# A two-layer diffusion trunk: the blocks of a triangular inverse through DRAM as diagonal halves in one orientation, and two modulation chunks on VectorE

## The chip, the cores and the metric

One core of a Trainium2 chip runs the whole program. The metric is device microseconds of one execution, the median of several runs. The core has five engines with a queue of instructions each, run in order: TensorE (PE, and PEld for its weight loads), VectorE (DVE), ScalarE (ACT), GpSimd (POOL) and SyncE (SP). SP, ScalarE and GpSimd also issue DMAs; sixteen DMA engines move the bytes.

## The reference, cut to what matters

A trunk of two layers over 256 positions of width 2048, beside 256 positions of context. The first layer mixes by windowed attention (8 query heads, 2 key-value heads) and by a gated delta rule (8 heads, two directions); the second by a Fourier transform. A gated feed-forward follows in both, and six modulation vectors per layer come from `c @ w_ada`. The delta rule solves a triangular system for each head, direction and chunk of the sequence:

```python
    m = jnp.where(strict, jnp.einsum('bhncd,bhnsd->bhncs', kb, kc) * decay, 0.0)
    rhs = jnp.concatenate([vc * bc[..., None], kb * jnp.exp(gc)[..., None]], axis=-1)
    sol = lax.linalg.triangular_solve(jnp.eye(DELTA_CHUNK, dtype=jnp.float32) + m, rhs,
                                      left_side=True, lower=True, unit_diagonal=True)
```

The first step of all is `mx = split(silu_c @ w_ada + b_ada)` and `h = modulate(rms_norm(x), mx[0], mx[1])`, for x and for the context.

## The kernel before, in words

**Matrix products.** Every weight tile is loaded by SP into `raw` (L188), split by ScalarE into a rounded part `whi` (L198) and by VectorE into the rest `wlo` (L204). TensorE multiplies both with the split activations (all its products are issued on L133). `raw` has 4 buffers, `whi` and `wlo` 4 each. The order on the queues is made by a scheduler that goes by the program's order; the program itself is paced by `clock[0]`, the time that the TensorE work issued so far should take. A generator that says `yield x` goes on once 1.2 x us of such work have been issued after it. So `yield` sets how much TensorE work lies between two steps.

**The front.** The first two modulation vectors of layer 0 are computed in 32 chunks (16 blocks k of 128 rows, shift and scale), each loaded in two halves. `WHO` says by a letter who does a chunk: `p`, TensorE with 8 products per half (each two instructions); `d`, VectorE with two multiply-and-reduce steps per half (L275), one for x and one for the context. `mod_k` (L447 to L455) then makes the modulated, split activations `hT` of block k, and `proj_k` multiplies them with the first weights. Chunks are issued two blocks ahead of `mod_k`, and `mod_k` one ahead of `proj_k`. The first product of a block in `proj_k` goes to 32 rows (`pab`). The other ten vectors (`ada_d`) are made by VectorE in the background, also on L275.

**The delta rule.** The heads are worked in four pairs g = 0 to 3, while the projections of the next pairs and of the attention run. `gdn_a(g)` builds the system `Z`, and copies its 32x32 diagonal blocks into `Zc` (L718 to L720, with a turn of direction 1's blocks by VectorE). The two 16x16 diagonal halves of each block are inverted by elimination on VectorE, with one half block per partition. To get from blocks laid over partitions to one half block per partition, `Zc` is stored to DRAM (`dz`, L722, ScalarE's queue) and read back in two loads (L731). The elimination (L737 to L742, 15 steps) makes `Y`. `Y` and its turned copy (L745) are stored to `dy` in four DMAs, two on ScalarE's queue and two on SP's (L750). `dy` is one DRAM tile for all pairs, cleared once at the start (L244 to L248), so that the halves off the diagonal are zero. `gdn_b(g)` reads both orientations back as whole blocks, `YD` (L762, ScalarE's queue), then reads Kt and Vt (L767, L768), and goes on with small 32x32 products: `pQ`, `pP` (the off-diagonal halves), and the larger blocks after them. In the profile `YZ` and `YD` have the name T (their buffers are T4).

**Attention.** `attend(0)` and `attend(1)` load the queries of a key-value head from DRAM on GpSimd's queue: `attend(0)` all four heads at once into an A buffer, `attend(1)` two and two into QCH buffers, which also hold the pairs' queries.

The change touches `WHO` (L60), the constants at L244, `gdn_a`, `gdn_b` and `attend`.

Of the kernel before, what the change touches and what calls it, by code (L numbers as in the profile page):

```python
# [58 lines left out]

WHO = 'pd' * 16  # L60
PRE = (4, 4, 4, 4)
# [11 lines left out]
def trunk(ctx: ExitStack, tc: tile.TileContext, a: dict, dbg=None, stop=None):  # L73
# [20 lines left out]
    def t4(shape, dt=F32):  # L94
        return T(shape, "T4", 2, dt)
# [147 lines left out]
    nc.gpsimd.dma_start(off16, a["k_off16"])  # L243
    dy = dr.tile([2, 2, 8, 4, 32, 32], F32, tag="dy", name="dy", bufs=1)  # L244
    zero = T([P, 512], "C2", 3)
    nc.gpsimd.memset(zero, 0.0)
    for i in range(2):
        nc.gpsimd.dma_start(dy[i].rearrange("d e b r c -> (d e b) (r c)").rearrange("a (b c) -> (a b) c", b=2), zero)  # L248
    smallr = C([P, 3, 16], "smallr")
# [383 lines left out]
    def bl(i, n=32):  # L633
        return slice(n * i, n * i + n)

    def gdn_a(g):
# [83 lines left out]
        V.transpose(Zc[:, 1].rearrange("p e f -> p (e f)"), Zd1.rearrange("p e f -> p (e f)"))  # L720
        dz = dr.tile([2, 8, 4, 32, 32], F32, tag="dz", name=f"dz{g}")
        S.dma_start(dz.rearrange("d e b r c -> (b r) (d e) c"), Zc.rearrange("p d e c -> p (d e) c"))  # L722
        YZ = t4([P, 4, 16, 16])
        Y2, Zi = YZ[:, 0:2], YZ[:, 2]
        Yf = Y2[:, 0].rearrange("p r c -> p (r c)")
        nc.gpsimd.memset(Yf, 0.0)
        nc.gpsimd.memset(Yf[:, 0:256:17], 1.0)
        yield LD1
        for s in range(2):
            sl = slice(16 * s, 16 * s + 16)  # L730
            S.dma_start(Zi[bl(s, 64)], dz[:, :, :, sl, sl].rearrange("d e b r c -> (d e b) r c"))  # L731

        V.tensor_tensor(out=Zc.rearrange("p d e c -> p (d e) c"), in0=Zc.rearrange("p d e c -> p (d e) c"),
                        in1=off16.unsqueeze(1).to_broadcast([P, 16, 32]), op=ALU.mult)
        yield LD2
        Y = Y2[:, 0]
        for k in range(15, 0, -1):  # L737
            tmp = YZ[:, 3].rearrange("p r c -> p (r c)")[:, (k % 4) * 64:(k % 4) * 64 + k * (16 - k)]
            tv = tmp.rearrange("p (r c) -> p r c", r=k)
            V.tensor_tensor(out=tv, in0=Zi[:, 0:k, k:k + 1].to_broadcast([P, k, 16 - k]),  # L740
                            in1=Y[:, k:k + 1, k:16].to_broadcast([P, k, 16 - k]), op=ALU.mult)
            V.tensor_tensor(out=Y[:, 0:k, k:16], in0=Y[:, 0:k, k:16], in1=tv, op=ALU.subtract)  # L742
            if k % 4 == 0:
                yield YSUB
        V.tensor_copy(Y2[:, 1], Y.rearrange("p r c -> p c r"))  # L745
        yield 1.5
        for i in range(2):
            for s in range(2):
                sl = slice(16 * s, 16 * s + 16)
                (S, nc.sync)[s].dma_start(dy[i][:, :, :, sl, sl].rearrange("d e b r c -> (d e b) r c"), Y2[bl(s, 64), i])  # L750
        heads.setdefault(g, {}).update(K=K, Q=Q, Z=Z, Zv=Zv, A=A, Zc=Zc, sc=(ner, dvs, so1, so2))

    def gdn_b(g):
# [7 lines left out]
        YD = t4([P, 2, 2, 8, 32])  # L761
        S.dma_start(YD.rearrange("p i d e c -> p (i d e) c"), dy.rearrange("i d e b r c -> (b r) (i d e) c"))  # L762
        if g == 0:
            Kt, Vt = H["Kt"], H["Vt"]
        else:
            Kt, Vt = ktok([P, 2, 4, HD]), vtok([P, 2, 4, HD])
            S.dma_start(Kt.rearrange("p h c d -> p h (c d)"), dKt[g])  # L767
            S.dma_start(Vt.rearrange("p h c d -> p h (c d)"), dVt[g])  # L768
        yield LD4
        pQ = sm()  # L770
        pQv = pQ.rearrange("p (d e f) -> p d e f", d=2, e=8)
# [232 lines left out]
    def attend(kv):  # L1004
        for hp in range(2):
            if kv == 0:
                if hp == 0:
                    q4 = at([P, 4, 256])
                    nc.gpsimd.dma_start(q4, dq[0])
                qT = q4[:, hp * 2:hp * 2 + 2]  # L1010
            else:
                qT = qch([P, 2, 256])
                nc.gpsimd.dma_start(qT, dq[kv][:, hp * 2:hp * 2 + 2])
            yield 3
# [519 lines left out]
```

## Time and profile before

| | us |
|---|---|
| median of 3 runs | 2500.32 (2495.74 to 2503.1) |
| profiled execution | 2498.01 |
| its span | 2496.2 |
| TensorE busy | 2382.9 (95%) |
| VectorE busy | 1791.7 (72%) |
| ScalarE busy | 1284.7 (51%) |

The front ends at about 185 us; the delta rule, the projections and the attention fill the time to about 750 us; the output projection, feed-forward, Fourier mixing and second feed-forward follow. In the rows below, a timeline row has start us, length us, engine, line, operation, out<-in, shapes, count, and in brackets the idle time before it and what ended it. A window row has the stretch, its length, the busy us of PE, PEld, DVE, ACT and POOL with their instructions, the granted TensorE clock (1.00 is full speed), the busy share of the DMA engines and GB/s. A row on waits has the engine and line that waited, what for, us in total, times, longest.

### The profile page before, as it was taken

The numbers are of one execution on the slowest core, as the hardware profiler recorded it, in microseconds if no ns is written. First come the engines' busy times: TensorE is split into PE (matmuls) and PEld (weight loads), VectorE is DVE, ScalarE is ACT, GpSimd is POOL, SyncE is SP. The second block draws the span as 40 slices with busy tenths as digits, with TensorE's granted clock in tenths as the row PEclk, the third lists the DMA queues.
The fourth block names the chain that finished last, engine by engine and source line by source line (L and its number), as shares of the span: only waits on it lengthen the run. The fifth ranks groups of instructions, "written<-read, shape, count | busy, mean of one in ns | idle before, by whom it ended". The sixth has DMA issues, their size and how long they took to land.

```text
span 2496.2 us, 39579 instructions
## 1 busy us (share of the span) xinstructions
PE 2382.9 (95%) x14536; PEld 1982.1 (79%) x14536; DVE 1791.7 (72%) x3379; ACT 1284.7 (51%) x2314; POOL 84.7 (3%) x106
## 2 busy tenths in 40 slices
PE   7999899988999999999999999799999999999997
PEld 6888688966778788888888887777888888888886
DVE  5889788877575787777777787878666666555566
ACT  5347345463755645444454545546554544445455
POOL 1000000000000100000000001002000000000001
PEclk8999999989999999999999999999999999999998
DMA  8885777668256589888888898586576777656665
GB/s 302 289 291 180 230 226 259 210 219 275 69 185 205 177 309 314 311 306 317 318 311 313 309 321 305 206 294 217 189 239 233 234 238 243 192 183 190 189 202 192
DMA packets 218483, 611.04 MB, mean 245 GB/s; under 512 B 68904, under 2 KB 69912, under 8 KB 217520
## 3 DMA queue, kind: packets, MB, share of 16 engines
q1 hardware_dynamic: 168016, 581.59, 68.4%
q10 hardware_dynamic: 46528, 15.21, 2.5%
q0 software_dynamic: 3744, 11.71, 1.4%
q8 instruction: 114, 1.87, 0.3%
q14 instruction: 81, 0.66, 0.1%
HBM read 595.03 MB, written 13.40 MB: 244 GB/s over the span
## 4 chain that ended last, share of the span: by engine, by line
PE 78%; DVE 8%; DMA 7%; ACT 3%; issue 3%; POOL 0%; ACTq 0%; DVEq 0%; POOLq 0%
PE acc L133 68%; PE sm L133 9%; DMA araw<-in_ada_d 3%; DVE wlo L204 2%; DVE araw L275 2%; DVE C L524 1%; DVE S L1169 1%; PE sm L1252 1%; DMA T<-dz 1%; DMA dy<-T 1%; DMA T<-dy 1%; ACT whi L198 1%; DMA araw<-in_w_dn 0%; DMA dz<-Zc 0%; DMA smallr<-in_smallr 0%
## 5 line engine op out<-in xcount | busy, mean ns | idle before, releaser
L198 ACT ACTIVATE whi<-raw 128x512 fp32r<-128x512 f32 (+1 forms) x1324 | 831.1, 630 | 895.7 <-DVE wlo L204 465.5
L204 DVE TENSOR_TENSOR wlo<-raw,whi 128x512 fp32r<-128x512 f32 (+1 forms) x1306 | 893.9, 692 | 482.9 <-ACT whi L198 480.3
L133 PE MATMUL acc<-whi,S 128*128 128x512 f32 x3312 | 1058.6, 397 | 6.6 <-ACT whi L198 5.4
L133 PEld LDWEIGHTS acc<-whi,S 128*128 128x128 f32 x3312 | 626.5, 189 | 142.8 <-ACT whi L198 5.8
L133 PE MATMUL acc<-wlo,S 128*128 128x512 f32 x1656 | 650.6, 393 | 2.0 <-DVE wlo L204 2.0
L275 DVE SCALAR_TENSOR_TENSOR araw<-araw,cb 128x1024 f32<-128x1024 f32 x320 | 389.1, 1218 | 33.8 <-DMA araw<-in_ada_d 33.1
L133 PEld LDWEIGHTS acc<-wlo,S 128*128 128x128 f32 x1656 | 313.6, 189 | 72.5 <-DVE wlo L204 3.4
L133 PE MATMUL acc<-S,whi 128*128 128x256 f32 x1152 | 221.3, 287 | 3.1 <-DVE C L524 3.0
L133 PEld LDWEIGHTS acc<-S,whi 128*128 128x128 f32 x1152 | 184.1, 192 | 4.0 <-issue 3.1
L133 PE MATMUL acc<-S,wlo 128*128 128x256 f32 x576 | 163.3, 284 | 2.0 <-DVE wlo L204 2.0
L133 PE MATMUL acc<-whi,ZT 128*128 128x512 f32 x384 | 122.0, 391 | 0.0
L133 PEld LDWEIGHTS acc<-S,wlo 128*128 128x128 f32 x576 | 110.8, 192 | 2.7 <-DVE wlo L204 2.6
L133 PE MATMUL acc<-whi,KCH 128*128 128x512 f32 x320 | 111.1, 404 | 1.1 <-ACT whi L198 1.1
L133 PE MATMUL acc<-whi,A 128*128 128x512 f32 x312 | 105.5, 393 | 0.0
L133 PE MATMUL acc<-whi,T 128*128 128x512 f32 x296 | 99.5, 392 | 0.0
L133 PE MATMUL acc<-wlo,KCH 128*128 128x512 f32 x192 | 78.7, 410 | 7.0 <-DVE wlo L204 6.8
L133 PEld LDWEIGHTS acc<-whi,ZT 128*128 128x128 f32 x384 | 72.2, 188 | 15.2
L133 PE MATMUL acc<-wlo,ZT 128*128 128x512 f32 x192 | 75.5, 393 | 0.2 <-POOL wlo L204 0.2
L133 PEld LDWEIGHTS acc<-whi,KCH 128*128 128x128 f32 x320 | 62.2, 195 | 15.1 <-ACT whi L198 1.5
L133 PE MATMUL acc<-wlo,T 128*128 128x512 f32 x176 | 68.9, 391 | 0.0
L133 PEld LDWEIGHTS acc<-whi,A 128*128 128x128 f32 x312 | 58.6, 188 | 11.9
L133 PEld LDWEIGHTS acc<-whi,T 128*128 128x128 f32 x296 | 55.6, 188 | 12.2
(442 smaller groups left out, 2638.0 us busy)
## 6 DMA issues: line engine op xcount, KB each, us to landing
raw<-in_w_gu SPq DMA_DIRECT2D x347, 512.0 KB, 4.3
araw<-in_ada_d SPq DMA_DIRECT2D x320, 512.0 KB, 4.8
raw<-in_w_dn SPq DMA_DIRECT2D x179, 512.0 KB, 4.6
raw<-in_w_att SPq DMA_DIRECT2D x40, 512.0 KB, 4.5
raw<-in_w_gdn SPq DMA_DIRECT2D x34, 512.0 KB, 4.6
raw<-in_w_out SPq DMA_DIRECT2D x30, 512.0 KB, 3.5
raw<-in_w_four SPq DMA_DIRECT2D x30, 512.0 KB, 4.3
ZT<-in_ada_s SPq DMA_DIRECT2D x24, 512.0 KB, 4.5
```

Of the source, the lines that this page charges most:

```text
L133: nc.tensor.matmul(out, l, r, start=start, stop=stop)
L198: S.activation(hi[:, :w], raw[:, c:c + w], AF.Copy)
L204: eng.tensor_sub(lo[:, :w], raw[:, c:c + w], hi[:, :w].bitcast(F32))
L275: V.scalar_tensor_tensor(out=junk, in0=w, scalar=1.0, in1=rows, op0=ALU.mult, op1=ALU.mult, accum_out=dst)
L524: V.scalar_tensor_tensor(out=ca[:, :, lo:hi], in0=pv[:, :, lo + o:hi + o], scalar=wconv[:, blk, j:j + 1], in1=ca[:, :, lo:hi], op0=ALU.mul ...
L1169: V.scalar_tensor_tensor(out=x[:, t, sl], in0=y[:, t, sl], scalar=r, in1=x[:, t, sl], op0=ALU.mult, op1=ALU.add)
L1252: nc.tensor.transpose(p[:, i * P:(i + 1) * P], hv[t][:, i * P:(i + 1) * P], ident)
```

## The change

The letters of `WHO` are changed so that chunks 12 and 28 (the shift of blocks 6 and 14) are `d` instead of `p`. `dy` is no longer cleared, and is one tile per pair; a constant of two columns, `half`, has 1 for partitions of a block's one half and 0 for the other, and the reverse. In `gdn_a` VectorE takes the diagonal halves out of `Zc` into `Zd`, the store carries these alone, and one load reads them, one contiguous row per partition. `Y` alone is stored, in one DMA on ScalarE's queue, without the turned copy and the pause of 1.5 before it. In `gdn_b` the load brings `Y`'s halves; ScalarE and VectorE write them into the two halves of the blocks with zeros beside them, and VectorE turns the blocks for the second orientation, with a pause of 1 after it. `attend(1)` loads its four heads at once, into a T4 buffer.

```diff
-WHO = 'pd' * 16
+WHO = ('pd' * 6 + 'dd' + 'pd') * 2
...
-    dy = dr.tile([2, 2, 8, 4, 32, 32], F32, tag="dy", name="dy", bufs=1)
-    zero = T([P, 512], "C2", 3)
-    nc.gpsimd.memset(zero, 0.0)
-    for i in range(2):
-        nc.gpsimd.dma_start(dy[i].rearrange("d e b r c -> (d e b) (r c)").rearrange("a (b c) -> (a b) c", b=2), zero)
+
+    half = C([P, 2], "half")
+    V.tensor_copy(half[:, 0:1], off16[:, 16:17])
+    V.tensor_scalar(half[:, 1:2], off16[:, 16:17], -1.0, 1.0, ALU.mult, ALU.add)
...
-        dz = dr.tile([2, 8, 4, 32, 32], F32, tag="dz", name=f"dz{g}")
-        S.dma_start(dz.rearrange("d e b r c -> (b r) (d e) c"), Zc.rearrange("p d e c -> p (d e) c"))
-        YZ = t4([P, 4, 16, 16])
-        Y2, Zi = YZ[:, 0:2], YZ[:, 2]
-        Yf = Y2[:, 0].rearrange("p r c -> p (r c)")
+        Zf = Zc.rearrange("p d e c -> p (d e) c")
+        Zd = T([P, 16, 16], "K1", 3)
+        V.tensor_scalar_mul(Zd, Zf[:, :, 0:16], half[:, 0:1])
+        V.scalar_tensor_tensor(out=Zd, in0=Zf[:, :, 16:32], scalar=half[:, 1:2], in1=Zd, op0=ALU.mult, op1=ALU.add)
+        dz = dr.tile([16, 4, 2, 16, 16], F32, tag="dz", name=f"dz{g}")
+        S.dma_start(dz.rearrange("e b s r c -> (b s r) e c"), Zd)
+        YZ = t4([P, 3, 16, 16])
+        Y, Zi = YZ[:, 0], YZ[:, 1]
+        Yf = Y.rearrange("p r c -> p (r c)")
...
-        for s in range(2):
-            sl = slice(16 * s, 16 * s + 16)
-            S.dma_start(Zi[bl(s, 64)], dz[:, :, :, sl, sl].rearrange("d e b r c -> (d e b) r c"))
+        S.dma_start(Zi.rearrange("p r c -> p (r c)"), dz.rearrange("e b s r c -> (e b s) (r c)"))
...
-        V.tensor_copy(Y2[:, 1], Y.rearrange("p r c -> p c r"))
-        yield 1.5
-        for i in range(2):
-            for s in range(2):
-                sl = slice(16 * s, 16 * s + 16)
-                (S, nc.sync)[s].dma_start(dy[i][:, :, :, sl, sl].rearrange("d e b r c -> (d e b) r c"), Y2[bl(s, 64), i])
+        dy = dr.tile([16, 4, 2, 16, 16], F32, tag="dy", name=f"dy{g}")
+        S.dma_start(dy.rearrange("e b s r c -> (e b s) (r c)"), Yf)
...
-        S.dma_start(YD.rearrange("p i d e c -> p (i d e) c"), dy.rearrange("i d e b r c -> (b r) (i d e) c"))
+        Yd = T([P, 16, 16], "K1", 3)
+        S.dma_start(Yd, H["dy"].rearrange("e b s r c -> (b s r) e c"))
...
         yield LD4
+        Yw = YD[:, 0].rearrange("p d e c -> p (d e) c")
+        S.activation(Yw[:, :, 0:16], Yd, AF.Copy, scale=half[:, 0:1])
+        V.tensor_scalar_mul(Yw[:, :, 16:32], Yd, half[:, 1:2])
+        V.transpose(YD[:, 1].rearrange("p d e c -> p (d e c)"), YD[:, 0].rearrange("p d e c -> p (d e c)"))
+        yield 1
...
-            if kv == 0:
-                if hp == 0:
-                    q4 = at([P, 4, 256])
-                    nc.gpsimd.dma_start(q4, dq[0])
-                qT = q4[:, hp * 2:hp * 2 + 2]
-            else:
-                qT = qch([P, 2, 256])
-                nc.gpsimd.dma_start(qT, dq[kv][:, hp * 2:hp * 2 + 2])
+            if hp == 0:
+                q4 = (at, t4)[kv]([P, 4, 256])
+                nc.gpsimd.dma_start(q4, dq[kv])
+            qT = q4[:, hp * 2:hp * 2 + 2]
```

## Rows read from the trace of the kernel before

**Rows 1.** Timeline of TensorE, the two stops at the inverse's load.

```profile
309.17 1.08 PE L133 MATMUL sm<-T,Zc 32*32 32x32 f32 x64 [7.07 <-DMA T<-dy]
...
507.59 0.64 PE L133 MATMUL sm<-T,Zc 32*32 32x32 f32 x28 [8.19 <-DMA T<-dy]
```

**Rows 2.** Waits of TensorE over the whole span.

```profile
PE acc L133 <- ACT whi L198: 6.5, 2, 5.4
PE sm L133 <- DMA QCH<-dq: 5.7, 1, 5.7
```

**Rows 3.** Windows of 10 us around the stops.

```profile
300.00:310.00 10.00, 2.93 (x71) 2.23 (x72) 6.26 (x12) 2.18 (x6) 0.44 (x2) 0.72 1.08 288
310.00:320.00 10.00, 10.00 (x186) 7.17 (x176) 6.32 (x15) 4.02 (x15) 1.16 (x2) 0.77 0.56 205
500.00:510.00 10.00, 2.41 (x36) 2.37 (x37) 4.39 (x9) 1.49 (x3) 0.00 (x0) 0.61 0.92 292
510.00:520.00 10.00, 10.00 (x49) 8.43 (x47) 5.83 (x15) 7.63 (x12) 0.00 (x0) 0.87 0.31 106
610.00:620.00 10.00, 5.56 (x10) 2.93 (x10) 5.15 (x9) 3.30 (x6) 1.29 (x2) 0.66 0.86 261
```

**Rows 4.** Windows over the pairs' stretch.

```profile
300.00:420.00 120.00, 106.09 (x1710) 99.21 (x1710) 101.52 (x240) 53.02 (x112) 6.47 (x13) 0.96 0.81 252
420.00:520.00 100.00, 85.96 (x890) 80.56 (x889) 79.11 (x198) 48.34 (x98) 0.97 (x3) 0.93 0.67 210
```

**Rows 5.** The front: a window, then timeline rows of TensorE and VectorE.

```profile
60.00:166.00 106.00, 106.00 (x900) 90.07 (x900) 86.61 (x183) 39.23 (x96) 0.00 (x0) 1.00 0.82 294
...
100.03 3.66 PE L133 MATMUL sm<-ZT,c2c 128*2 128x128 f32 x32
...
107.97 1.22 DVE L275 SCALAR_TENSOR_TENSOR E<-ZT,cb 128x1024 bf16<-128x1024 f32 x1 [0.46 <-DMA ZT<-in_ada_s]
...
168.43 0.75 DVE L455 TENSOR_TENSOR S<-E,S 128x256 fp32r<-128x256 f32 x2
...
175.94 0.28 PE L133 MATMUL sm<-S,wlo 128*32 128x256 f32 x1
```

**Rows 6.** Chain of waits at the head (start us, us, what).

```profile
5.14 8.69 DMA smallr<-in_smallr
```

**Rows 7.** Landing times of lines 722 (store dz), 731 (read dz), 762 (read dy).

```profile
DMA to landing us min/median/max: 3.2/4.0/6.2
...
DMA to landing us min/median/max: 3.1/5.1/12.3
...
DMA to landing us min/median/max: 6.2/8.4/14.5
```

**Rows 8.** DMA issues: count, KB each, median us to landing.

```profile
dQ<-C ACTq DMA_DIRECT2D x6, 128.0 KB, 4.0
...
dy<-T ACTq DMA_DIRECT2D x8, 64.0 KB, 5.7
...
A<-dq POOLq DMA_DIRECT2D x1, 512.0 KB, 8.7
QCH<-dq POOLq DMA_DIRECT2D x2, 256.0 KB, 4.0
```

**Rows 9.** Lines 745 and 720 on VectorE: ns min/median/max.

```profile
L745 DVE COPY T<-T x4: 367/374/376, 296.4 to 591.6; 128x256 f32<-128x256 f32 x4
...
L720 DVE STREAM_TRANSPOSE Zc<-K x4: 433/439/439, 263.7 to 562.8; 128x256 f32<-128x256 f32 x4
```

**Rows 10.** Chain of waits: read of dz (pair 0), read of dy (pair 2).

```profile
268.73 12.21 DMA T<-dz
...
497.31 10.15 DMA T<-dy
```

**Rows 11.** Timeline of ScalarE near 600 us, pair 3.

```profile
599.96 12.18 ACTq L768 DMA_DIRECT2D VTOK<-dVt  x1
...
612.24 0.63 ACT L198 ACTIVATE whi<-raw 128x512 fp32r<-128x512 f32 x1 [10.68 <-issue]
```

More of the change, by code (lines that the diff above doesn't have):

```diff
@@ L735, in gdn_a @@
         yield LD2
-        Y = Y2[:, 0]
         for k in range(15, 0, -1):
-            tmp = YZ[:, 3].rearrange("p r c -> p (r c)")[:, (k % 4) * 64:(k % 4) * 64 + k * (16 - k)]
+            tmp = YZ[:, 2].rearrange("p r c -> p (r c)")[:, (k % 4) * 64:(k % 4) * 64 + k * (16 - k)]
             tv = tmp.rearrange("p (r c) -> p r c", r=k)
@@ L744, in gdn_a @@
                 yield YSUB
-        V.tensor_copy(Y2[:, 1], Y.rearrange("p r c -> p c r"))
-        yield 1.5
-        for i in range(2):
-            for s in range(2):
-                sl = slice(16 * s, 16 * s + 16)
-                (S, nc.sync)[s].dma_start(dy[i][:, :, :, sl, sl].rearrange("d e b r c -> (d e b) r c"), Y2[bl(s, 64), i])
-        heads.setdefault(g, {}).update(K=K, Q=Q, Z=Z, Zv=Zv, A=A, Zc=Zc, sc=(ner, dvs, so1, so2))
+        dy = dr.tile([16, 4, 2, 16, 16], F32, tag="dy", name=f"dy{g}")
+        S.dma_start(dy.rearrange("e b s r c -> (e b s) (r c)"), Yf)
+        heads.setdefault(g, {}).update(dy=dy, K=K, Q=Q, Z=Z, Zv=Zv, A=A, Zc=Zc, sc=(ner, dvs, so1, so2))
     def gdn_b(g):
```

## The prediction

> **What bounds the kernel now.** I read the waits of TensorE first, because TensorE is busy for almost the whole span: what the change can win is either a stop of TensorE or work taken from it. Two of its longest stops have the same name, the load of the inverse from DRAM: 7.07 us at 302 us and 8.19 us at 499 us [rows 1]. A third, 5.4 us, waits for ScalarE's whi, and a fourth, 5.7 us, for the queries of the second key-value head [rows 2]. Next I read windows around these stops for the granted clock: it is 0.72 and 0.77 in the two windows at the first stop, 0.61 and 0.87 at the second, 0.66 at the third [rows 3], between the chip's two levels of 1.2 and 2.4 GHz, so each stop costs a little more than its length. Then I read the chain of waits and the landing times, to see which transfer is late, and last VectorE's load between 300 and 520 us, because that engine would be the next bound: 101.5 of 120 us and 79.1 of 100 us [rows 4].
>
> **The front: two chunks from TensorE to VectorE.** Between 60 and 166 us TensorE is busy for all 106 us, VectorE for 86.6 [rows 5]. One chunk on TensorE is 32 instructions, 3.66 us [rows 5]; two of them go, 7.3 us. VectorE gets four multiply-and-reduce steps of 1.22 us per chunk [rows 5], 4.9 us. The first extra chunk belongs to block 6; VectorE has some 19 us without work in this stage, and I cost it at nothing. The second belongs to block 14, and there the margin is thin: the last hT of block 14 is written at 169.2 us (168.43 + 0.75), and TensorE begins that block's projection at about 175.9 us, a margin of 6.7 us [rows 5]. With TensorE 7.3 us earlier and VectorE at worst 4.9 us later, TensorE waits 5.5 us at worst, and 0.6 us if VectorE's idle time takes in the extra chunk. I take 2.5 us, near the middle. The front gives -4.8 us (-6.7 to -1.8).
>
> **The head.** The clearing of dy goes, a memset and two stores of 256 KB from GpSimd. The load of smallr, on the chain of waits with 8.69 us from 5.14 us on [rows 6], stands among them and lands a little sooner. Two constant columns on VectorE replace it, beside waits for loads. I take -1 us (-2 to 0).
>
> **The blocks through DRAM, per head pair.** The pieces can be counted in the code. Before: 2048 of 128 bytes written to dz, 2048 of 64 bytes read, 4096 of 64 bytes written to dy, 4096 of 128 bytes read; 12288 in all. After: 2048 of 64 bytes, 128 of 1 KB, 128 of 1 KB, 2048 of 64 bytes; 4352. The new store of dz has as many pieces as the old one, 4.0 us in the median (3.2 to 6.2) [rows 7], and I leave it at that. The nearest row to a transfer with 128 pieces of 1 KB is the store of dQ, 128 KB, 4.0 us against 5.7 us of the old dy stores [rows 8]. For the read of dz that is now one contiguous row per partition I take 3.4 us; the old one took 3.1 to 12.3 us [rows 7]. The read of dy took 6.2 to 14.5 us, median 8.4 [rows 7]; with half the pieces I take 4.5 us, bounds 3.1 (the shortest read with 64-byte pieces) and 8.4.
>
> A rule of the Trainium skill (DMA: Bandwidth & Descriptors, "Why small descriptors are slow") says that a piece costs its beats of 32 bytes plus about 3 cycles. By that an estimate for the new read is 8.4 x (2048 x 5) / (4096 x 7) = 3.0 us, and the sum would be 1.5 us smaller at the second stop. The same page's specifications table counts anything under 512 bytes as read-modify-write, which speaks against halving the pieces of the dz store; the rows with 64-byte stores show 5.7 us with 4096 pieces under way, no slower per piece than the 128-byte ones.
>
> VectorE gets two more steps over 128x256 on the way out, one more plus a 32x32 turn over 512 elements on the way in, and loses one copy. With 0.37 us for a copy and 0.44 us for a turn of 256 elements [rows 9] that is 3 x 0.4 + 0.9 - 0.4 = 1.7 us per pair, 6.8 us in all; ScalarE gets one step of the same size and issues two DMAs fewer per pair, SP two fewer. On the path of the inverse the new steps add about 0.8 us before the store and 1.4 us after the load (ScalarE and VectorE write one half each, then the turn).
>
> **First stop (pair 0, 302 us).** The read of dz took 12.21 us [rows 10]; at 3.4 us it is 8.8 us earlier. VectorE stood idle for most of that time, so its elimination starts earlier too. With 2.0 us from the dy store and 1.7 us from the read, less 2.2 us of new steps, the inverse is ready 10.3 us sooner than at 309.2 us, or 298.9 us. TensorE asks at 302.1 us, less the 1.8 us of the pause taken out, plus the 1.2 us of the new one. The 7.07 us go. At the clock of the two windows 2.93 x 0.28 + 10.0 x 0.23 = 3.1 us come back [rows 3]. Together -10.2 us (-11.9 to -5).
>
> **Second stop (pair 2, 499 us).** Here VectorE is the slower one before the store: its elimination is interleaved with other work, so I let only 1 us of the faster dz read through, which the new steps use up. The gains are 1.7 us at the store and 10.15 - 4.5 = 5.6 us at the read [rows 10], the losses 1.4 us for the half copies and the turn, and 1 to 2 us because these wait in VectorE's queue. TensorE's 8.19 us become 3.7 us (2.4 to 8): -4.5 us. Of the clock's 2.41 x 0.39 + 10.0 x 0.13 = 2.2 us [rows 3] half comes back. Together -5.6 us (-8 to 0).
>
> **Third stop (pair 3, 600 us).** ScalarE's issue of the load of Vt took 12.18 us, 0.6 us after the read of dy was issued with its 4096 pieces; ScalarE's next whi begins 10.68 us late [rows 11], and TensorE stops for 5.4 us [rows 2]. No other issue on ScalarE's queue takes as long, those behind the 2048 pieces of a dz store included, so I expect this stop to go: -5.4 us, and 5.56 x 0.34 = 1.9 us of clock [rows 3]. But the fourth stop follows at once. The queries are written on GpSimd's queue and read back by it; TensorE arrives 5.4 us sooner, and so do the queries, because ScalarE copies them sooner. Their load now brings 512 KB instead of 256 KB: 8.7 us against 4.0 us in the two rows there are [rows 8], the former beside the 4096 pieces. I take +1 us (0 to 4.7). Together -6.3 us (-7.3 to -1.5). The buffer is another (T4), last used by pair 3's own elimination and free by then. The second load that waited on GpSimd for pair 3's queries goes; TensorE did not wait for it.
>
> **What is added elsewhere.** At pairs 1 and 3 TensorE had no stop at the inverse; the steps in front of it may now cost 0.7 us each, 1.5 us. VectorE's 6.8 us lie on an engine that is 79 to 85% busy [rows 4]; I let 1.5 us through (0 to 6.8). Queued behind the new waits: on ScalarE the splits of the weights stand behind the half copy, on VectorE the wlo behind the other half, and TensorE waits for both. Together +3 us.
>
> **Sum.** -1 - 4.8 - 10.2 - 5.6 - 6.3 + 3 = -24.9 us. The profiled execution took 2498.0 us, so 2473.1 us; the median of the runs lies 2.3 us above it. Forecast **2475 us**. The best ends give -2 - 6.7 - 11.9 - 8 - 7.3 = -35.9, or 2464 us.
>
> **Rivals.** (1) *VectorE takes the place of the DMAs.* Between 300 and 520 us it is busy for 180.6 of 220 us [rows 4]; with TensorE some 16 us faster over the same stretch and 5 us of new steps it would be at 91%, and in an in-order queue TensorE would then stop for wlo, the elimination and the turns. For it: only 1 us of the second pair's delay is idle time of VectorE. Against it: at the first stop VectorE itself stood waiting. Half of the pairs' 22.1 us would be left, the front at its worst end: -1 - 1.8 - 11 + 3 = -10.8, **2489 us**.
>
> (2) *ScalarE and VectorE stand where TensorE stood* (slower). Before, only TensorE waited for the read of dy. Now the half copies on ScalarE and VectorE do, and weights stop behind them. The ScalarE stop of 10.7 us cost TensorE 5.4 us, so 5.3 us had cover; the clock cost 2 to 3 us per stop. If the half copy is queued right behind the store, it stands for store and read. At pair 0's old times for these, about 12.2 us, that is 12.2 - 5.3 + 3 = 9.9 us per pair, 39.6 us for four, against 24.9 us won: +14.7, **2515 us**. It decides from 24.9 / 4 + 2.3 = 8.5 us of standing per pair, which is the forecast of store and read together, so the place of the half copy in the queue matters. Against it: the code lets 7.2 us of TensorE's work pass between the issue of the read and the half copies, and the read should take 4.5 us.
>
> (3) *Nothing moves by more than a few us*, because the new order of work on the queues gives back at the end of the stage, in the drain before the output projection, what the pairs win: **2498 us**.
>
> **How the numbers follow.** Forecast 0.63, rival 1 0.21, rival 2 0.07, rival 3 0.09. 0.3% is 7.5 us, about what a measurement of this kernel tells from no change. Faster than 2492.8 us are the forecast and most of rival 1: 0.80; within 0.3% the rest of rival 1 and rival 3: 0.13; slower rival 2: 0.07. The range reaches from just under the best ends to just above rival 3: 2461 to 2502 us.
>
> **What would show it.** Right: no TensorE wait for the read of dy above 4 us; no issue of a DMA on ScalarE longer than 2 us near pair 3; the read of dz at 3 to 4 us at every pair; TensorE's instructions 64 fewer for the chunks; a wait for the queries of 5 to 8 us that stays. Wrong: new TensorE waits for Y or the turn of 3 us or more at each pair (rival 1), ScalarE waiting for dy in front of whi for more than 5 us (rival 2), a longer stretch of low load before the output projection (rival 3), or TensorE waiting for hT at 165 to 180 us by more than 5 us.

## The result, and the profile after

The changed kernel is slower. Its median is 2521.94 us over 4 runs (2518.23 to 2525.44) against 2498.03 us for the kernel before: ratio 1.0096, 95% interval 1.0075 to 1.0116, or +23.9 us where -24.9 us were predicted. The profiled span is 2516.3 us.

The head of the page after: span, busy time and share, number of instructions of the engines.

```profile
span 2516.3 us, 39435 instructions
...
PE 2408.9 (96%) x14470; PEld 1981.7 (79%) x14470; DVE 1802.2 (72%) x3409; ACT 1285.9 (51%) x2314; POOL 82.0 (3%) x102
```

TensorE has 66 instructions fewer than before, as the change of the chunks says, and yet is busy for 26.0 us more (2408.9 against 2382.9). That is the first hint: the time did not go into waiting. The chain of waits says where it went (start us, us, what). First the kernel before:

```profile
841.73 40.19 PE acc L133 x175
...
927.63 43.96 PE acc L133 x192
...
1840.41 43.96 PE acc L133 x192
```

and the kernel after:

```profile
835.13 40.90 PE acc L133 x175
...
922.57 44.80 PE acc L133 x192
...
1851.49 44.81 PE acc L133 x192
```

The first of these blocks of the feed-forward begins 6.6 us earlier than before. From there on the kernel before needs 1654.5 us to its end, the kernel after 1681.2 us. The blocks of 192 products in the chain take 44.80 to 44.84 us instead of 43.96, without a wait inside them and at a granted clock of 1.00 in both. Nothing in the diff touches these products.

The stretch that the prediction was about, from the waits of TensorE between 300 and 640 us in the kernel after:

```profile
PE sm L133 <- DMA T<-dq: 6.0, 1, 6.0
PE sm L133 <- DVE T L770: 5.8, 1, 5.8
...
PE sm L133 <- DMA A<-dq: 2.1, 1, 2.1
```

Both stops at the load of dy [rows 1] are gone under that name. One of them, at pair 0, has become a stop of 5.76 us for VectorE's turn (L770); the one at pair 2 is gone, and so is the stop for whi [rows 2]. The stop for the queries stays, under the name of the new load. The landing times of the four DMAs of a pair, in the order dz store, dz read, dy store, dy read (L725, L732, L746, L759):

```profile
DMA to landing us min/median/max: 3.0/4.3/6.3
...
DMA to landing us min/median/max: 2.1/3.9/5.3
...
DMA to landing us min/median/max: 3.7/4.3/5.4
...
DMA to landing us min/median/max: 3.6/4.4/5.8
```

So the medians came near to what the prediction wanted (4.0, 3.4, 4.0 and 4.5 us): those of the reads were 5.1 and 8.4 us before [rows 7].

### The profile page after: what moved, and what is told of

Its sections match the earlier page's. It is cut to its first block, busy times and chain, and to the rows that moved or that the text cites. A ratio compares the mean times of both kernels' runs of the same rounds, so it can differ in the third digit from the quotient of the medians.

```text
span 2516.3 us, 39435 instructions
## 1 busy us (share of the span) xinstructions
PE 2408.9 (96%) x14470; PEld 1981.7 (79%) x14470; DVE 1802.2 (72%) x3409; ACT 1285.9 (51%) x2314; POOL 82.0 (3%) x102
## 4 chain that ended last, share of the span: by engine, by line
PE 76%; DVE 10%; DMA 6%; ACT 4%; issue 3%; POOL 0%; DVEq 0%; ACTq 0%; SPq 0%; POOLq 0%
PE acc L133 69%; PE sm L133 6%; DMA araw<-in_ada_d 2%; DVE E L274 2%; DVE araw L274 2%; DVE wlo L204 2%; DVE S L1167 1%; PE sm L1250 1%; DVE C L523 1%; ACT whi L198 1%; DMA dy<-T 1%; DMA dz<-K 1%; DMA K<-dy 1%; DMA T<-dz 0%; DMA smallr<-in_smallr 0%
## 5 line engine op out<-in xcount | busy, mean ns | idle before, releaser
L133 PE MATMUL acc<-wlo,S 128*128 128x512 f32 x1656 | 658.3, 398 | 0.3 <-DVE wlo L204 0.2
```

Source lines behind the costliest of these rows:

```text
L133: nc.tensor.matmul(out, l, r, start=start, stop=stop)
```

## What changed without being in the diff: places in SBUF

An address is that of the compiled program, in bytes within a partition. `half` is a new tile of 8 bytes and takes 32, and the ring C2 is first used at a later point, so that it moves behind other tiles. With that, whi moves from 191296 to 191328 and wlo from 199488 to 199520 (from 64 to 96 above a multiple of 256). T4, A, KCH and ZT go from a multiple of 256 to 192 above one, KTOK from 192 to 128; S, the tile of split activations in the blocks shown above, stays at a multiple of 256. The first four runs ask whether that is the cause. Each leaves the work as it is and only adds unused bytes.

**Run e1: the kernel after, 32 more bytes.**

```diff
     dg = c2([P, 2, 2, P])
+    padt = C([P, 8], "padt")
+    nc.gpsimd.memset(padt, 0.0)
```

> The changed kernel with 32 unused bytes per partition put in front of OG, araw, raw, whi and wlo. In the changed kernel these tiles start 32 bytes past a multiple of 64, since half takes 32 bytes; here they start on a multiple of 64 again, as in the kernel before. Theory A (the place of whi and wlo costs 4.4 ns per product over 512 columns): the feed-forward's 192 products take 43.96 us instead of 44.80, and the run about 2493 us, 29 less than the changed kernel. Theory B (the slower products come with the changed order of work or with the chip, not with the place): 44.80 us and 2522 us stay.

Measured: 2510.67 us, ratio 1.0044 (1.0029 to 1.0059); 44.62 us in most blocks, 44.79 in others. The places matter, but a multiple of 64 is not what heals them.

**Run e2: the kernel before, the same 32 bytes.** The same two lines in the kernel before.

> The kernel before with 32 unused bytes at the same place, so that OG, araw, raw, whi, wlo and what follows start 32 bytes past a multiple of 64. Theory A: 44.80 us for 192 products of the feed-forward and about 2527 us, 29 more than before. Theory B: 43.96 us and 2498 us.

Measured: 2523.51 us, ratio 1.0089 (1.0064 to 1.0114). The chain of waits of this run has the loss of the kernel after, with nothing of the change in it:

```profile
925.98 44.81 PE acc L133 x192
```

**Runs e3 and e4: whi and wlo moved apart, in the kernel before.** In e3 (the edit below) 32 unused bytes stand ahead of whi and 32 ahead of wlo; in e4 32 stand ahead of wlo and 32 behind it, and whi keeps its place.

```diff
+                if nload[0] == 1 and c == 0:
+                    nc.gpsimd.memset(C([P, 8], "pad1"), 0.0)
                 hi = T([P, 512], "whi", 4, F32R)
+                if nload[0] == 1 and c == 0:
+                    nc.gpsimd.memset(C([P, 8], "pad2"), 0.0)
                 lo = T([P, 512], "wlo", 4, F32R)
```

> The kernel before with only whi moved by 32 bytes; raw, wlo and all else keep their place in 64 bytes. Two thirds of the products stream whi. Theory A, the product's own read is slower: two thirds of the loss, some 19 us, about 2517 us, and 44.5 us for 192 products. Theory C, it is the load into raw, or another tile behind: 2498 us.

> The kernel before with only wlo moved by 32 bytes. One third of the products stream wlo. Theory A: one third of the loss, some 10 us, about 2508 us, and 44.2 us for 192 products. Theory C: 2498 us.

Measured: e3 (whi at 96, wlo at 128 above a multiple of 256) 2522.23 us, 1.0083 (1.0056 to 1.0109), 44.80 us per block; e4 (64 and 96) 2509.91 us, 1.0045 (1.003 to 1.0059), 44.38 us per block. With wlo alone out of its place half of the loss is there, with both all of it; and for wlo, with whi at 96, 128 is no better than 96, though it is a multiple of 64.

**Run e5: the kernel after, every tile where the kernel before has it.** The two columns of `half` go into unused bytes of gnorm's slot, and the tile of zeros is allocated and filled as before, but written nowhere.

```diff
-    half = C([P, 2], "half")
+    zero = T([P, 512], "C2", 3)
+    nc.gpsimd.memset(zero, 0.0)
...
-    gnorm = C([P, 1], "gnorm")
+    gh = C([P, 3], "gnorm")
+    gnorm, half = gh[:, 0:1], gh[:, 1:3]
```

> The kernel after, with nothing of its work changed, but with every tile at the address that it has in the kernel before: the two small factors go into the two unused columns of the gain's slot, and the tile that the kernel before fills with zeros is still allocated (and filled, but written to nowhere), so that the ring it belongs to stands where it stood. whi at 191296 and wlo at 199488 again. Theory A (the place of whi and wlo sets the rate of their products): the blocks of 192 products take 43.96 us as in the kernel before, the first of them begins at about 835 us as in the kernel after (against 841.7 before), and what follows takes before's 1654.5 us: span 835.1 + 1654.5 = 2489.6, a median of about 2491.5, ratio to the kernel before 0.997. Rival (something else of the change slows the products): 44.80 us and 2522, ratio 1.0096.

Measured: 2486.40 us against 2496.58 for the kernel before in the same set, ratio 0.9958 (0.9944 to 0.9973). The chain of waits:

```profile
828.06 40.16 PE acc L133 x175
...
913.93 43.95 PE acc L133 x192
...
1830.72 43.96 PE acc L133 x192
```

The blocks have the old rate again. The change itself wins 10.2 us (6.7 to 14.0); in its own places it loses them and 23.9 us more.

## Which places are good

One group of products is two with whi and one with wlo. In these products TensorE loads a 128x128 piece of the activations (S here, in other blocks A, KCH, ZT, T or KTOK), and the 512 columns of whi or wlo move past it; the trace has the load as a row of its own, here in the kernel before:

```profile
927.70 0.42 PEld L133 LDWEIGHTS acc<-whi,S 128*128 128x128 f32 x2
```

Below, "weights" are whi and wlo, the tiles that move, and "activations" the tile that is loaded; the expectations of e13 and e16 call that one the moving tile. The time of a group can be read from one wlo product to the next on TensorE's timeline (start us, length us). The kernel before, then the kernel after:

```profile
927.70 0.40 PE L133 MATMUL acc<-wlo,S 128*128 128x512 f32 x1
928.39 0.39 PE L133 MATMUL acc<-wlo,S 128*128 128x512 f32 x1
929.08 0.39 PE L133 MATMUL acc<-wlo,S 128*128 128x512 f32 x1
```

```profile
924.05 0.39 PE L133 MATMUL acc<-wlo,S 128*128 128x512 f32 x1
924.75 0.39 PE L133 MATMUL acc<-wlo,S 128*128 128x512 f32 x1
925.45 0.39 PE L133 MATMUL acc<-wlo,S 128*128 128x512 f32 x1
```

0.69 and 0.70 us here; 0.687 and 0.700 us as means over a block (43.96 / 64 and 44.80 / 64).

**Runs e7 and e8: the kernel before with 64 and with 128 unused bytes** (the lines of e1 with 16 and 32 columns).

> The kernel before with 64 unused bytes between its first and its later tiles: whi at 191360 and wlo at 199552, both multiples of 64 and of 128 (before: 64 above a multiple of 128). If all that counts is a multiple of 64: 43.96 us per 192 products and 2498, ratio 1.000. If the place within 128 bytes counts, as the padded kernel after suggests (44.62 at the same places): 44.6 to 44.8 us, and 2518 to 2524, ratio 1.008 to 1.010.

> The kernel before with 128 unused bytes there: whi at 191424 and wlo at 199616, 192 above a multiple of 256 (before: 64 above), but 64 above a multiple of 128 as in the kernel before. If the place repeats every 128 bytes: 43.96 us per 192 products and 2498, ratio 1.000. If it repeats every 256 bytes or not at all: 44.6 to 44.8 us and 2518 to 2524.

Measured: 2524.30 us, 1.0111 (1.0088 to 1.0135), blocks of 44.62 and 44.79 us; and 2521.55 us, 1.0099 (1.0076 to 1.0123), 44.80 us. Neither a multiple of 64 nor a period of 128 is the rule.

**Runs e9 to e11: buffers of whi at different places.** The stride between the four buffers of whi is made larger, so that a single run has four places. A step below is four groups of products (two with whi, one with wlo) with one buffer of each.

```diff
-                hi = T([P, 512], "whi", 4, F32R)
+                hi = T([P, 520], "whi", 4, F32R)[:, 0:512]
```

In e11 520 is 576; in e9 128 unused bytes stand behind whi, in e10 128 ahead of it.

> The kernel before with the four buffers of whi 2080 bytes apart instead of 2048, so that consecutive steps of one block of products read their first parts at 64, 96, 128 and 160 bytes above a multiple of 256 (191296, 193376, 195456, 197536); wlo at 199744, 64 above a multiple of 256 as before, but 256 bytes further on. If only the place of each tile within 256 bytes counts: steps with the first buffer keep 0.687 us for a group of two whi products and one wlo product, the other three show about 0.694 (whi's half of the loss), a block of 192 takes about 44.3 us. If 256 bytes further on is already another place: no step shows 0.687.

> As the scan before it, the four buffers of whi at 192, 224, 0 and 32 above a multiple of 256 (191424, 193504, 195584, 197664), wlo at 199744. Theory of a place within 256 bytes: all four steps near 0.694 us; if one of them is below 0.687, there is a better place than that of the kernel before, and the kernel with whi and wlo there should beat it.

> The kernel before with the four buffers of whi 2304 bytes apart (191296, 193600, 195904, 198208) and wlo 1024 bytes further on (200512): all at 64 above a multiple of 256. Theory of a place within 256 bytes: 0.687 us in all four steps and 43.96 us per 192 products. If the place within 512 bytes counts: the second and the fourth buffer slow (0.694). If the distance to another tile or an absolute place counts: slow with all but the first buffer, or with all.

Measured, one run each: 2514.73, 2509.91 and 2500.93 us. In e11, with whi 0, 256, 512 and 768 bytes and wlo 1024 bytes further on, the blocks take 43.96 us: what counts repeats every 256 bytes. In e9 one step in four took 0.690 to 0.695 us per group in most blocks, the others up to 0.6975, a block 44.48 to 44.51 us; in e10 no step over S was below 0.6925 and blocks took 44.57 to 44.59. No place of whi was better than the old one.

**Run e13: the kernel after with 224 unused bytes** (56 columns in the lines of e1). Weights at 64 above a multiple of 256 again, ZT, A, T4 and KCH still at 192.

> The kernel after with 224 unused bytes behind its first tiles: whi at 191552 and wlo at 199744, 64 above a multiple of 256 again, while the tiles that other blocks of products read as their moving side (T4, A, KCH, ZT) stay where the kernel after has them, 192 above a multiple of 256 instead of 0. If the weights' own place within 256 bytes decides: 43.96 us per 192 products, the means of the products that read ZT, A and T as in the kernel before (391 to 394 ns), and a median near 2487 to 2491, ratio 0.996. If the distance between the weights and the moving tile decides: 43.96 us for the blocks over S, but 396 to 398 ns for those over ZT, A and T, and a median some 4 us higher.

Measured: 2497.23 us, ratio 0.9997 (0.9984 to 1.0010). This run showed the other half of the rule. Timeline of TensorE in one execution, first a block over S, then one over ZT; three wlo products are left out between the two rows of each, so that four groups lie between them:

```profile
1029.70 0.39 PE L133 MATMUL acc<-wlo,S 128*128 128x512 f32 x1
...
1032.45 0.39 PE L133 MATMUL acc<-wlo,S 128*128 128x512 f32 x1
...
1110.09 0.40 PE L133 MATMUL acc<-wlo,ZT 128*128 128x512 f32 x1
...
1112.89 0.39 PE L133 MATMUL acc<-wlo,ZT 128*128 128x512 f32 x1
```

2.75 / 4 = 0.6875 us over S, 2.80 / 4 = 0.70 us over ZT, with the same buffers of weights. So I sorted the groups of all runs by the distance of the weights from the activations, counted within 256 bytes. The times are means over 21 or more groups of one tile between 1095 and 1290 us; whi and wlo lie at the same place within 256 bytes in all of these:

| weights minus activations | us per group | seen in |
|---|---|---|
| 0 | 0.684 | e1 and e8, over KTOK |
| 64 | 0.687 | before, e5, e11 over S, A, KCH, ZT, T; e13 over S |
| 96 | 0.700 | e2 over S, A, KCH, ZT, T; after over S |
| 128 | 0.697 to 0.700 | e7 over S, A, KCH, ZT, T; e13 over A, KCH, ZT, T; e1 over S; before over KTOK |
| 160 | 0.703 | after over A, KCH, ZT, T; e2 over KTOK |
| 192 | 0.700 | e8 over S, A, KCH, ZT, T; e1 over A, KCH, ZT, T; e7 and e13 over KTOK |
| 224 | 0.699 | after over KTOK |

**Runs e16 and e18: all distances at 0.** Three groups of unused bytes put whi, wlo, S, T4, A, KCH, ZT and KTOK at multiples of 256; e16 in the kernel of e5, e18 in the kernel before.

```diff
+    nc.gpsimd.memset(C([P, 16], "pad1"), 0.0)
     ccb = [ktok([P, 1024]), vtok([P, 1024])]
+    nc.gpsimd.memset(C([P, 48], "pad2"), 0.0)
...
     dg = c2([P, 2, 2, P])
+    nc.gpsimd.memset(C([P, 48], "pad3"), 0.0)
```

> The kernel after with its tiles in their old places, but for three groups of unused bytes (64, 192 and 192) that put whi, wlo and all the tiles that move past them (S, T4, A, KCH, ZT, KTOK) at multiples of 256. In the traces so far a group of two whi products and one wlo product takes 0.684 us where weights and moving tile lie at the same place within 256 bytes (KTOK at 192 with weights at 192, KTOK at 128 with weights at 128), 0.687 us at a distance of 64, and 0.697 to 0.703 us at 96, 128, 160, 192 and 224. If the distance decides: 0.684 us in all blocks, 64 x 0.684 = 43.8 us per 192 products, KTOK's blocks 0.684 instead of 0.700, and a median of about 2479, 6 to 8 us below the kernel with the old places. The rival is the scan with whi at 0 and wlo at 64, where no group was below 0.69: if a place of 0 is bad by itself, 44.6 us per 192 products and a median above 2505.

> The kernel before with the same three groups of unused bytes, so that weights and moving tiles all lie at multiples of 256, and nothing else. Between the two kernels with the change, the places were worth 16.7 us (2486.4 to 2469.7). If places and change add up: 2498 - 16.7 = 2481, ratio 0.993, with 43.55 us per 192 products. If the stops of the kernel before give part of it back: 2484 to 2490.

Measured: e16 2469.73 us, ratio 0.9888 (0.9870 to 0.9906), a version that beats both kernels by more than 1%; e18 2483.71 us, 0.9946 (0.9931 to 0.9961). Timeline of TensorE in e16:

```profile
923.84 0.39 PE L133 MATMUL acc<-wlo,S 128*128 128x512 f32 x1
924.52 0.39 PE L133 MATMUL acc<-wlo,S 128*128 128x512 f32 x1
925.20 0.39 PE L133 MATMUL acc<-wlo,S 128*128 128x512 f32 x1
```

and its chain of waits:

```profile
918.32 43.54 PE acc L133 x192
...
1824.60 43.55 PE acc L133 x192
```

0.680 us per group over every tile, KTOK's too (0.700 before): a little less than the 0.684 that I expected. Each measured against the kernel before of its own set, the places are worth 19.0 us between e5 and e16 (-10.2 and -29.2) and 14.1 us in e18; they add to the change's own gain.

A distance of 0 is not the best one for every product. In the front and in the projections of the pairs the roles are the other way round: TensorE loads 128x128 pieces of whi and wlo, and 256 columns of S move past them. Timeline of TensorE, the kernel before and then e18, one group apart:

```profile
181.72 0.28 PE L133 MATMUL acc<-S,wlo 128*128 128x256 f32 x1
182.06 0.28 PE L133 MATMUL acc<-S,wlo 128*128 128x256 f32 x1
```

```profile
181.25 0.28 PE L133 MATMUL acc<-S,wlo 128*128 128x256 f32 x1
181.61 0.28 PE L133 MATMUL acc<-S,wlo 128*128 128x256 f32 x1
```

As means over some 480 groups, these take 0.347 us in the kernel before (weights minus S: 64), 0.355 in the kernel after (96) and 0.359 in e16 and e18 (0). So e18 comes to its first product of 128x512 later than the kernel before (248.44 against 243.39 us, of which 0.8 us are in the head), and wins only behind it. No run gives each of the two shapes the distance that suits it.

Two things stay open. Why the distance counts, no trace here shows. And where whi and wlo lie at different places the table is not enough: in e10 the step with whi at 0 and wlo at 64 should have taken under 0.69 us over S by it, and no step did. In e9 one step in four has whi and wlo at the places within 256 bytes that gave 0.687 us in the kernel before, and the fastest step took 0.690 to 0.695 in most blocks. No rule for mixed places is shown.

## What the change itself is worth

**Run e12: e5 without the two chunks in front.**

```diff
-WHO = ('pd' * 6 + 'dd' + 'pd') * 2
+WHO = 'pd' * 16
```

> The kernel after with its tiles in their old places, without the two chunks that VectorE takes over in front (every second chunk by TensorE again, as before). The front's own gain, read as 6.1 us between the traces, should be lost: the conv after the front again at about 188.9 us, and a median of about 2492.5, ratio 0.9983. The rival, that the front's time is taken up by the waits for dz and dy behind it, expects 2487 and 0.996.

Measured: 2493.35 us against 2497.05, ratio 0.9989 (0.9974 to 1.0005). By the medians the chunks carry most of the change's gain (10.2 - 3.7 = 6.5 us, uncertain by some 5 us; in the traces the first product of 128x512 comes at 237.95 us in e5 and at 244.23 in e12, 6.3 us apart); the blocks' way through DRAM and the queries together give 3.7 us (by the interval from a loss of 1.2 to a gain of 6.5), where the prediction had 19.1.

**Run e14: e5 without the wait for the inverse.** dy is loaded but not used; the blocks are built from a constant.

```diff
-        S.activation(Yw[:, :, 0:16], Yd, AF.Copy, scale=half[:, 0:1])
-        V.tensor_scalar_mul(Yw[:, :, 16:32], Yd, half[:, 1:2])
+        Yc = ident[:, 0:16].unsqueeze(1).to_broadcast([P, 16, 16])
+        S.activation(Yw[:, :, 0:16], Yc, AF.Copy, scale=half[:, 0:1])
+        V.tensor_scalar_mul(Yw[:, :, 16:32], Yc, half[:, 1:2])
```

> The kernel after with its tiles in their old places; the half blocks that come back from DRAM are loaded, but not used: the factor of the inverse is built from a constant tile, so that no engine waits for the elimination, the store and the read (the inversion's result is left out of the computation). If the stops at the inverse still cost what TensorE's waits show (7.4 us at pair 0, under 1 us at the others, and the clock behind it), the median falls by 8 to 11 us to about 2477. If VectorE's queue bounds the stretch and the stop only shows it, it falls by less than 3 us. If it falls by more than 14 us, the round trips cost more than the waits say.

Measured: 2477.82 us against 2497.93, ratio 0.9908 (0.9893 to 0.9922): 20.1 us below the kernel before, 9.9 us more than e5. The stop that is left at the inverse, 7.43 us at pair 0 in e5, is worth its length and the clock behind it. So it is the path of the inverse that holds up TensorE there, and not the load of VectorE, which this run leaves nearly as it was.

**Runs e15 and e17: the queries by two loads again,** in the places of e5 and of e16. The diff's last part is undone.

> The kernel after with its tiles in their old places, with the queries of the second key-value head loaded by two loads again, as in the kernel before. The one load lands 6.6 us after its issue and TensorE waits 6.3 us for it, the old one was waited for by 5.7 us, so I expect nothing that can be told from noise: 2484 to 2489. The rival, by the prediction (the load beside it costs more because it is larger), expects 2 to 4 us less: 2482 to 2484; if the one load saved TensorE's second wait, 5 us more: 2491.

> As the run with all distances at 0, with the queries of the second key-value head loaded by two loads again. If what the old loads seemed to give (2.5 us between two runs of different sets of executions) is real and adds up: 2 to 3 us below that run, about 2476. If it was noise: the same as that run within 1.5 us.

Measured: 2483.91 us, ratio 0.9934 (0.9920 to 0.9949), and 2469.01 us, 0.9884 (0.9865 to 0.9903). Against its own set e15 gains 14.0 us where e5 gained 10.2; beside e16, in one set, e17 is 0.7 us faster. So the one load of the later queries gives nothing here, and whether it costs 1 to 4 us these runs do not settle.

**Run e6: e5 with the exponential of the small row emitted behind the projections.**

```diff
     ea = C([P, 16], "ea")
-    V.tensor_copy(ea, exp_fine(smallr[:, 1, :], [P, 16]))
...
+    V.tensor_copy(ea, exp_fine(smallr[:, 1, :], [P, 16]))
     abT = e2([32, 512])
```

> As the run with the tiles in their old places, and one more edit: the exponential of the small row (ea), which the schedule had put ahead of the broadcast copies on ScalarE's queue, is emitted only where the gates are worked out, behind the projections. The theory that this order costs the head 4.4 us expects the first modulation copies at 30.3 us instead of 34.7, the stretch before the feed-forward 3 to 4.4 us shorter and a median of about 2487.5, ratio 0.9957. The rival, that the head's loss is swallowed by the wait for the chunks' DMAs behind it, expects no more than 1 us.

Measured: 2486.17 us, ratio 0.9952 (0.9935 to 0.9969), the same as e5. The premise fell: the head's 4.4 us had gone already in e5, whose first products over the copies of the context start at 29.87 us (30.32 before, 34.70 after). The edit had nothing left to win.

## Why the prediction was wrong, step by step

**The step that is missing.** The head was costed by instructions alone: two constant columns for a cleared tile, -1 us. That a new tile moves all tiles behind it stands nowhere in the sum, in no rival and in no bound, and it decides the sign. With the head, it is the 34.1 us between e5 (-10.2) and the kernel after (+23.9). Most of it can be counted from the page. The products of TensorE with wlo and 512 columns, one for each group, in the kernel after (busy us, mean ns of one):

```profile
L133 PE MATMUL acc<-wlo,S 128*128 128x512 f32 x1656 | 658.3, 398 | 0.3 <-DVE wlo L204 0.2
...
L133 PE MATMUL acc<-wlo,KCH 128*128 128x512 f32 x192 | 78.2, 408 | 8.1 <-DVE wlo L204 7.9 <-POOL wlo L204 0.2
L133 PE MATMUL acc<-wlo,ZT 128*128 128x512 f32 x192 | 76.4, 398 | 0.1
L133 PE MATMUL acc<-wlo,T 128*128 128x512 f32 x176 | 70.0, 398 | 1.3 <-DVE wlo L204 1.3
...
L133 PE MATMUL acc<-wlo,A 128*128 128x512 f32 x128 | 51.3, 401 | 5.0 <-DVE wlo L204 4.7 <-POOL wlo L204 0.2
```

1656 groups over S by 0.013 us (0.700 - 0.687) and 688 over the other four by 0.016 us (0.703 - 0.687) make 21.5 + 11.0 = 32.5 us. The 128x256 products are not in this count: 576 groups over S by 0.008 us (0.355 - 0.347) would be 4.6 us more. What is left of the measured times after the other terms is 29.7 us:

| term | predicted | measured | from |
|---|---|---|---|
| front | -4.8 | -6.5 | e5 against e12 |
| head | -1 | +4.4 | first products over the context at 34.70 instead of 30.32 us |
| stops and additions (-10.2 - 5.6 - 6.3 + 3) | -19.1 | -3.7 | e12 against the kernel before |
| places | not in the sum | +29.7 | remainder of +23.9; 32.5 by counting 128x512 groups |

The split between head and places is not shown by a run of its own. In e13, whose 128x256 groups take 0.347 us as in the kernel before, the head is 3.9 us late, but the first product of 128x512 only 2.0 us (239.96 against 237.95 us in e5); so part of the head's 4.4 us may not reach the end, and the places would then be worth more.

The same count gives e13: KCH, ZT, T and A at a distance of 128 (688 x 0.010 = 6.9 us) and the head (its first products over the context start at 33.74 us, 3.9 us later than in e5) are 10.8 us, or 8.9 with the 2.0; against their own sets e13 gains 9.5 us less than e5.

**The front** was right in kind and, by the medians, too small: 6.5 us is nearly all of the 7.3 us that TensorE gives away [rows 5], so the margin at block 14 does not seem used up.

**The head** went the other way. ScalarE's timeline in the kernel after:

```profile
4.28 1.28 ACT L337 ACT_TABLE_LOAD   x1
14.55 0.22 ACT L337 ACTIVATE K<-smallr 128x16 f32<-128x16 f32 x1 [8.99 <-DMA smallr<-in_smallr]
14.68 0.58 ACT L263 ACTIVATE cb<-sm 128x512 f32<-128x512 f32 x1
```

The scheduler put the exponential of smallr first on ScalarE's queue, ahead of the broadcast copies of cb. It stands for the load for 8.99 us, and TensorE waits 4.7 us for cb. In the kernel before, the squares of one tile and two copies stand ahead of it, and ScalarE stands for 2.56 us. Nor did smallr land sooner: the exponential begins at 14.55 us, before at 13.85. The prediction costed the removal of the stores and not the new order of the queue. This reading is from the traces; no run changes the order alone in a kernel that has the loss. The runs that keep the old places of the tiles with the tile of zeros have no such loss; the three with `half` as a tile of its own (the kernel after, e1, e13) start these products at 33.7 to 34.7 us.

**The first stop** is the term of the own gain that was most off: -10.2 us predicted, about 0 in the traces. The path of pair 0, from the timelines and chains:

| us | before | after | e12 (old front, old places) |
|---|---|---|---|
| store of dz issued | 264.15 | 268.16 | 268.29 |
| read of dz issued (in before, the later of two) | 268.73 | 274.49 | 273.71 |
| elimination begins | 281.06 | 278.81 | 279.84 |
| store of dy issued (in before, the later of two) | 296.77 | 295.60 | 297.29 |
| read of dy issued | 302.87 | 300.41 | 299.68 |
| TensorE goes on | 309.17 | 307.77 | 309.44 |

The read of dz takes 4.23 instead of 12.21 us, as predicted, but the store ahead of it is issued 4 us later and lands after 6.25 us. VectorE's timeline of the kernel after shows why, at both ends of the path:

```profile
265.79 0.44 DVE L719 STREAM_TRANSPOSE Zc<-K 128x256 f32<-128x256 f32 x1
...
266.72 0.35 DVE L722 TENSOR_SCALAR K<-Zc,half 128x256 f32<-128x256 f32 x1
266.98 0.68 DVE L204 TENSOR_TENSOR wlo<-raw,whi 128x512 fp32r<-128x512 f32 x1
267.58 0.48 DVE L723 SCALAR_TENSOR_TENSOR K<-Zc,half,K 128x256 f32<-128x256 f32 x1
...
304.57 0.35 DVE L769 TENSOR_SCALAR T<-K,half 128x256 f32<-128x256 f32 x1 [4.90 <-DMA K<-dy]
304.84 1.22 DVE L274 SCALAR_TENSOR_TENSOR araw<-araw,cb 128x1024 f32<-128x1024 f32 x1
...
306.92 0.70 DVE L770 STREAM_TRANSPOSE T<-T 128x512 f32<-128x512 f32 x1
```

Ahead of the store, the turn of direction 1's blocks starts at 265.79 us instead of 263.68, because a background dot and a split of weights got in front of it; another split stands behind it; and the two new steps of 0.35 and 0.48 us become 1.3 us because a third stands between them. Behind the read, the turn starts 2.35 us after the half copy before it because a background dot and two other steps got in between. The prediction added 2.2 us for the new steps by their own lengths; the table has some 4 us ahead of the store and 3 us behind the read. The elimination takes 16.7 us in the kernel after and 17.4 in e12 against 14.8 before; the prediction took its length as unchanged.

**The second stop** is gone, but that was not worth its length: TensorE reaches pair 2's first inverse product at 510.56 us in e5, 3 us later than before [rows 1], though it had passed pair 0's 6.5 us earlier. More products now stand ahead of it: TensorE is busy for 52.4 of the last 54.2 us there, against 41.4 of 51.0 before. **The third stop**: the long issue on ScalarE [rows 11] is gone (the longest DMA issue there is 1.06 us) and TensorE no longer stops for whi, but it stops 6.0 us and 2.1 us for the queries, and the window from 610 to 620 us has a clock of 0.50 where it had 0.66 [rows 3]. From pair 0's first inverse product to pair 3's, the kernel of e5 takes 322.3 us against 328.9 before: -6.6 us where -8.9 were predicted (-5.6 - 6.3 + 3). That looks near, but a single trace does not tell it well: with the same work there, e12 takes 316.3 us and e6 325.0.

**What was to show it.** Right were the missing wait for dy, the short issues on ScalarE, TensorE's 64 instructions fewer (66) and the wait for the queries that stays (6.0 us). The read of dz has a median of 3.9 us, but took 2.1 to 5.3 us and not 3 to 4 at every pair. Of the signs of a wrong forecast two came, each at one pair of four: a TensorE wait for the turn of more than 3 us (pair 0), and ScalarE waiting for dy for more than 5 us with a whi behind it (pair 1):

```profile
359.85 0.51 ACT L768 ACTIVATE T<-K,half 128x256 f32<-128x256 f32 x1 [7.76 <-DMA K<-dy]
```

TensorE did not wait for a whi there. No sign was named for the loss that came.

**The rivals.** Rival 1 priced the kernel without the loss of the places best (2489 us against 2486.4 of e5) and named its sign, a TensorE wait for the turn, but its sum had another make-up (-1.8 us in front), so the near number is luck. Rival 2 had the right sign for the wrong reason: in the kernel after ScalarE stood 2.60 us ahead of pair 0's half copy and 7.76 us ahead of pair 1's, VectorE 4.90 us ahead of pair 0's, all under the 8.5 us from which it decides; e5, where ScalarE stood 9.39 us at pair 1, is faster than the kernel before. The range's upper end, 2502 us, covered only what the diff showed.

**The rule weighed there.** The Trainium skill (DMA: Bandwidth & Descriptors, "Why small descriptors are slow") led to an estimate of 3.0 us for the new read of dy. The trace has a median of 4.4 us, so the row decides for the 4.5 us. The stores of dz with 64-byte pieces land after 4.3 us in the median against 4.0 us with as many of 128 bytes [rows 7]; the pieces of both are under the other rule's 512 bytes, so no run here shows what that rule costs.

## What to carry to other kernels

Where a change adds, removes or reorders tiles, list the addresses of the weight tiles and of the tiles that they are multiplied with, before and after, and cost a shift like any other edit: here 32 bytes outweighed everything else in the diff. When a profile shows the same blocks of products at the same clock with another length, look at the places first, and test them with a few unused bytes in the kernel before, each shape of product by itself: the two shapes here want different distances. A step that is put into the path of a transfer costs its place in its engine's queue, not its length alone.

## What the runs showed of the hardware

Not expected: the rate of products of 128x512 depends on the distance in bytes, within 256, between the tile that moves (here the weights) and the tile whose pieces are loaded (here the activations). A group of three took 0.680 us with both weights and every activation tile at multiples of 256 (0.684 over KTOK at the same distance of 0, but at 128 and 192 above a multiple), 0.687 at a distance of 64 and 0.697 to 0.703 at 96 to 224, at a granted clock of 1.00; that is 43.54 to 44.84 us per 192 products. Groups of 128x256 products, which load the weights and move S, went the other way: 0.359 us at 0 and 0.347 at 64. For the same work, the kernel before, the places make 2483.71 us in e18 and 2523.51 in e2, or 1.6% (1.4% by the ratios to the kernel before in their own sets).
